# Order of two products, of a minimum and of two sums in the paired projections of a hybrid GLA and convolution block

## The chip, the cores and the metric

The kernel runs on one core of one Trainium2 chip. The metric is the device time of one execution in microseconds (us). The version before takes 891.07 us as the median of three runs (890.15 to 894.06).

## The reference

One layer on x of 1024 tokens by 1024 features: RMSNorm, one input projection, a gated linear attention group (4 heads, both directions) and a short convolution group side by side, one output projection, a residual and a last RMSNorm. Cut to what matters here:

```python
h = rmsnorm(x, norm_g)
q, k, v, z_a, lr_f, lr_b, b_gate, c_gate, h_c, z_c = split(h @ w_in)
g_f = log_sigmoid(lr_f @ w_gk_f + b_gk_f) / 16      # log decays; g_b alike
b = cumsum(g, within chunks of 64)                  # inside the attention
u = c_gate * h_c
conv = conv_w[0] * up[:, :-2] + conv_w[1] * up[:, 1:-1] + conv_w[2] * up[:, 2:] + conv_b
y_c = b_gate * conv * silu(z_c)
```

## The kernel before, in words

All matmuls work on float32 that is split in two parts: `split` (L153, L154) makes the high part as a cast on ScalarE (`a_hi`) and the low part as a subtraction on GpSimd (`a_lo`), and each product takes three matmuls (high by high, low by high, high by low). `part` allots the two tiles and calls `split`.

The projections go by **pairs**: `pair` takes two blocks of 128 columns of `w_in` (`raw0`, `raw1`, each 1024 x 128, loaded by `weights` at L82 from SP's queue into a pool of four buffers named `raw`) and makes both results (128 x 1024 each, in two halves of 512 tokens) by a scheme of seven products instead of eight: sums of quarters of the weights (`comb`, L422, on VectorE), their splits (`os1` to `os4`, `o11`), seven products with quarters and sums of the tokens' matrix (`b00`, `b10`, `b11`, `t1` to `t4`), and additions of the results (`plus`, L445, on VectorE from PSUM, and L458). Each finished half is handed to `take(e, half, ap)`. The products use three PSUM banks in turn, `pa`, `pb` and `pc`.

Two pairs make a **quad**: `second` first computes a smaller scheme of the same kind for both (L519 to L556) on half banks `bx`, `by`, `bz`, `bw`. In it the bank `by` is written by a first product, added to `p1` (L542) and then written again by a second product; `bx` is copied at L540 and then gets its second product. L526 to L530 are the sums of the weights that it needs, from the first raw blocks of both pairs.

After some stages for the attention's values (up to about 115 us) eight conv quads run, j from 0 to 7, and then four quads for q, k and z (up to about 600 us); attention and output projection follow. In conv quad j, pair a gives C and hc: `conv_u`'s `take` multiplies them on GpSimd to u (L625) as soon as both have the same half. Pair b gives z and B: at its first result both halves of the convolution are made (L633 on ScalarE, L634 and L635 on VectorE); z's halves go through a tanh (L647, ScalarE) and L648, L649 (VectorE), B's through a product on GpSimd (L651); the finished half is stored (L654).

At the end of conv quad j, `gates` makes the log decays of one head and direction: two small matmuls (L591) into a bank `out`, from there |x| (L592, ScalarE) and min(x, 0) (L593, VectorE), then Exp (L594). `summed` loads another activation table and takes Ln (L601), and puts five steps into the list `beside`: a subtraction (L611) and a scan (L605 or L607) for each half, and the store to `b_dram` (L613). `step`, called after each `plus` of pair a of the next quad, takes one step from the list and places it behind that addition.

The order of the instructions on each engine is not the order of the text: a scheduler sets it from the priorities and dependencies, and `tc.issue_after(x)` tells it to place what follows behind x. L396 is the matmul of `product`.

Of the kernel before, what the change touches and what calls it, by code (L numbers as in the profile page):

```python
# [2 lines left out]

# [11 lines left out]
ALU = mybir.AluOpType  # L15
# [3 lines left out]
P = 128  # L19
# [18 lines left out]
def tile_hybrid_gla_shortconv(ctx, tc, x, norm_g, w_in, w_gk_f, b_gk_f, w_gk_b, b_gk_b,  # L38
                              gla_norm_g, conv_w, conv_b, w_out, final_g, out):
    nc = tc.nc  # L40
    V, A, G, T = nc.vector, nc.scalar, nc.gpsimd, nc.tensor
# [18 lines left out]
    b_dram = [[dram.tile([P, S], F32, name=f"b_dram{h}{d}") for d in range(2)] for h in range(NH)]  # L60
# [146 lines left out]
    def part(src, e_lo=G, late=False):  # L207
        pool, name, bufs = (resp, "w", 2) if late else (ws, "a", 6)
        hi, lo = (pool.tile([P, 4, P], F32R, name=f"{name}_{i}", bufs=bufs) for i in ("hi", "lo"))
        hi, lo = (a[:, 0:src.shape[1]] for a in (hi, lo))  # L210
        split(hi, lo, src, A, e_lo)
        return hi, lo
# [20 lines left out]
    with tc.manual_schedule():  # L233
# [24 lines left out]
        for t in range(NT):  # L258
            ps = bank()[:, 0:DV]
# [13 lines left out]
            if t == 1:  # L273
                a00, a01 = (load_a(2, i) for i in range(2))
            if t in (5, 6):
                w_next.append(split_v(v_raw1[t - 5]))
            if t == 6:
                a10, a11 = (load_a(3, i) for i in range(2))
# [107 lines left out]
    def tmp():  # L386
        return wk.tile([P, 512], F32, name="tmp", bufs=9)
# [17 lines left out]
    def load(col):  # L405
        return weights(w_in[:, :, col:col + P])


    beside = []
# [4 lines left out]
            with tc.issue_after(behind.ins):  # L414
                beside.pop(0)()

    def pair(raw0, raw1, take, c2=None, mid=None, step=lambda behind: None):

        a00, a01, a10, a11 = raw0[:, 0:4], raw0[:, 4:8], raw1[:, 0:4], raw1[:, 4:8]

        def comb(f, x0, x1, op):
            V.tensor_tensor(f, x0, x1, op)  # L422
            return f

        def t4_():
            return tmp().rearrange("p (c e) -> p c e", e=P)

        o00 = part(a00)
        if c2 is None:
            o01 = part(a01)  # L430
        s1 = comb(s_tile(), a10, a11, ALU.add)
        s2 = comb(s_tile(), s1, a00, ALU.subtract)
        os2 = part(s2)
        os3 = part(comb(t4_(), a00, a10, ALU.subtract))
        os1 = part(s1)
        o11 = part(a11)
        os4 = part(comb(t4_(), a01, s2, ALU.subtract))

        def whole_product(a, b_):
            ps = bank6()  # L440
            product(ps, a, b_, True, True)
            return ps

        def plus(f, ps, x):
            step(V.tensor_tensor(f, ps, x, ALU.add))  # L445
            return f

        pa = whole_product(o00, b00)
        p1 = tmp()
        A.copy(p1, pa)  # L450
        if mid is not None:
            mid()
        if c2 is None:
            product(pa, o01, b10, False, True)
            c2 = tmp()
            A.copy(c2, pa)
        else:
            V.tensor_tensor(c2, pa, c2, ALU.add)  # L458
        take(0, 0, c2)
        plus(p1, whole_product(os2, t2), p1)  # L460
        w = plus(tmp(), whole_product(os3, t3), p1)
        p5 = whole_product(os1, t1)
        take(1, 1, plus(tmp(), p5, w))
        plus(p1, p5, p1)
        take(1, 0, plus(w, whole_product(o11, t4), w))
        take(0, 1, plus(p1, whole_product(os4, b11), p1))

    def value_pair(h0, h1, o00, o01, os2, a00, a01, a10, a11, s2, beside):

# [49 lines left out]
    def second(x, y, h):  # L519

        b00, t1, t2, t3, b10, b11, t4 = h
        a00, a01, a10, a11 = x[:, 0:2], x[:, 2:4], y[:, 0:2], y[:, 2:4]
        f, g = s_tile(), s_tile()
        s2, s1, s3, s4 = f[:, 0:2], f[:, 2:4], g[:, 0:2], g[:, 2:4]
        o0 = part(x)
        V.tensor_tensor(s1, a10, a11, ALU.add)  # L526
        V.tensor_tensor(s2, s1, a00, ALU.subtract)
        o1 = part(f)
        V.tensor_tensor(s3, a00, a10, ALU.subtract)
        V.tensor_tensor(s4, a01, s2, ALU.subtract)  # L530
        o2 = part(g)
        o3 = part(a11)
        first_, last_ = (lambda o: tuple(a[:, 0:2] for a in o)), (lambda o: tuple(a[:, 2:4] for a in o))
        r = [wk.tile([P, 512], F32, name="r2", bufs=2) for _ in range(2)]
        lo, hi = slice(0, 256), slice(256, 512)
        w = tmp()
        p1, u = w[:, lo], w[:, hi]
        bx, by, bz, bw = (bank6()[:, lo] for _ in range(4))
        product(bx, first_(o0), b00, True, True)
        A.copy(p1, bx)  # L540
        product(by, first_(o1), t2, True, True)
        V.tensor_tensor(p1, by, p1, ALU.add)  # L542
        product(bz, first_(o2), t3, True, True)
        V.tensor_tensor(u, bz, p1, ALU.add)
        product(bw, last_(o1), t1, True, True)
        V.tensor_tensor(r[1][:, hi], bw, u, ALU.add)
        product(bx, last_(o0), b10, False, True)
        A.copy(r[0][:, lo], bx)
        product(by, o3, t4, True, True)
        V.tensor_tensor(r[1][:, lo], by, u, ALU.add)  # L550

        def finish():
            product(bw, last_(o2), b11, False, True)
            V.tensor_tensor(r[0][:, hi], bw, p1, ALU.add)

        return *r, finish  # L556

    def quad(cols_a, take_a, cols_b, take_b):
        xa, xb = load(cols_a[0]), load(cols_b[0])
        ra, rb, finish = second(xa[:, 4:8], xb[:, 4:8], h2)  # L560
        pair(xa, load(cols_a[1]), take_a, ra, finish, step)
        pair(xb, load(cols_b[1]), take_b, rb)

    def to_dram(dsts):
# [17 lines left out]
    def gates(h, d):  # L582

        bias = bgk[:, d, h:h + 1]
        dr = slice(d * 64, d * 64 + 64)
        b, m = u_tile()[:, 0:S], u_tile()[:, 0:S]
        for half in range(2):
            sl = slice(half * 512, half * 512 + 512)
            ps = bank()
            for i, w in enumerate((gk_hi, gk_lo)):  # L590
                T.matmul(ps, w[dr, h * DK:(h + 1) * DK], lr[half][dr], start=i == 0, stop=i == 1)  # L591
            A.activation(b[:, sl], ps, AF.Abs, bias=bias)  # L592
            V.tensor_scalar(m[:, sl], ps, bias, 0.0, ALU.add, ALU.min)  # L593
        return b, m, A.activation(b, b, AF.Exp, scale=-1.0)  # L594

    def summed(h, d, b, m, exp):

        with tc.issue_after(exp.ins):  # L600
            A.activation(b, b, AF.Ln, bias=1.0)  # L601

        def scan(b_, m_):
            if d == 0:
                V.tensor_tensor_scan(b_, smask, m_, 0.0, ALU.mult, ALU.add)  # L605
            else:
                V.tensor_tensor_scan(b_[:, ::-1], smask, m_[:, ::-1], 0.0, ALU.mult, ALU.add)  # L607

        for half in range(2):
            b_, m_ = (a[:, half * 512:half * 512 + 512] for a in (b, m))  # L610
            beside.append(lambda b_=b_, m_=m_: V.tensor_tensor(m_, m_, b_, ALU.subtract))  # L611
            beside.append(lambda b_=b_, m_=m_: scan(b_, m_))
        beside.append(lambda: nc.sync.dma_start(b_dram[h][d], b))  # L613

    def conv_u(j):
        u = u_tile()
# [451 lines left out]
```

## Time and profile before

| | us |
|---|---|
| median of three runs | 891.07 (890.15 to 894.06) |
| the profiled execution | 889.61 |
| its span | 887.9 |
| TensorE (PE) busy | 860.0 (97%) |
| VectorE (DVE) busy | 704.4 (79%) |
| GpSimd (POOL) busy | 421.6 (47%) |
| ScalarE (ACT) busy | 393.7 (44%) |

The span is what the profiler recorded of the profiled execution; the 1.7 us around it belong to the same execution's time. Busy shares are averages over the whole span, which has stages of different kinds; what holds in a stage is read from windows and timelines of that stage. An idle time in square brackets behind a row tells how long the engine had been idle and what released it. The granted clock of TensorE was 0.995 of full speed over the execution.

### The profile page before, as it was taken

How to read it: one execution, taken by the hardware profiler on the slowest of the kernel's cores; microseconds unless marked ns; L12 is line 12 of the kernel's file. 1: busy time of each engine (PE TensorE's matmuls, PEld its weight loads, DVE VectorE, ACT ScalarE, POOL GpSimd, SP SyncE). 2: the span in 40 equal slices, each digit the busy share in tenths (PEclk: the TensorE clock that was granted, in tenths of full speed). 3: DMA queues.
4: the chain of work that ended last, by engine and by line, in shares of the span. 5: the costliest groups of instructions: out<-in, count | busy, mean ns of one | idle time of the engine just before them, and what ended most of it. 6: DMA issues, size and time to landing. Idle time of an engine off the chain costs nothing.

```text
span 887.9 us, 12975 instructions
## 1 busy us (share of the span) xinstructions
PE 860.0 (97%) x4452; PEld 722.8 (81%) x4452; DVE 704.4 (79%) x1301; ACT 393.7 (44%) x823; POOL 421.6 (47%) x374
## 2 busy tenths in 40 slices
PE   7999989999999999999999999999999999999996
PEld 6999978887787878788878888887878787888885
DVE  5889968788888798888887566667799989975754
ACT  4634323454636263444544233433455446542453
POOL 3423657586767675766766554520112222222231
PEclk9999999999999999999999999999999999999998
DMA  8511331223132322222244433469665434410122
GB/s 301 115 54 49 96 120 48 82 62 118 49 95 72 96 66 77 72 72 72 72 132 129 131 96 105 135 210 392 226 205 190 131 113 135 131 37 24 42 78 95
DMA packets 102164, 100.35 MB, mean 113 GB/s; under 512 B 10705, under 2 KB 82385, under 8 KB 101586
## 3 DMA queue, kind: packets, MB, share of 16 engines
q1 hardware_dynamic: 102098, 99.53, 35.4%
q8 instruction: 35, 0.57, 0.3%
q14 instruction: 31, 0.25, 0.1%
HBM read 71.20 MB, written 28.31 MB: 112 GB/s over the span
## 4 chain that ended last, share of the span: by engine, by line
PE 76%; DVE 17%; issue 3%; DMA 2%; ACT 1%; SPq 0%; POOLq 0%; POOL 0%; DVEq 0%; ACTq 0%
PE out L734 16%; PE pa L396 16%; PE pb L396 15%; PE pc L396 15%; PE po L891 4%; PE out L223 3%; PE pu L936 2%; DVE tmp L445 1%; DVE tmp L649 1%; DVE s L422 1%; DVE tmp L320 1%; DMA b<-b_dram 1%; PE out L291 1%; DMA xt<-in_x 1%; PE pk L928 1%
## 5 line engine op out<-in xcount | busy, mean ns | idle before, releaser
L154 POOL TENSOR_TENSOR a_lo<-s,a_hi 128x512 fp32r<-128x512 f32 x74 | 116.2, 1575 | 54.8 <-ACT a_hi L153 54.5
L154 POOL TENSOR_TENSOR a_lo<-raw,a_hi 128x512 fp32r<-128x512 f32 x84 | 111.0, 1325 | 22.1 <-ACT a_hi L153 18.4
L154 POOL TENSOR_TENSOR a_lo<-tmp,a_hi 128x512 fp32r<-128x512 f32 x48 | 70.3, 1464 | 103.9 <-ACT a_hi L153 84.6
L148 POOL TENSOR_TENSOR rs<-rs,mhalf 128x1 f32<-128x1 f32 x48 | 28.7, 598 | 143.1 <-DVE rs L147 135.7
L734 PE MATMUL out<-a_hi,y_hi 128*128 128x512 f32 x192 | 88.7, 462 | 0.5 <-ACT y_hi L153 0.5
L153 ACT CAST a_hi<-raw 128x512 fp32r<-128x512 f32 x108 | 63.8, 596 | 56.4 <-PE pc L396 15.1
L153 ACT CAST a_hi<-tmp 128x512 fp32r<-128x512 f32 x48 | 29.8, 620 | 120.2 <-DVE tmp L422 98.9
L734 PE MATMUL out<-a_hi,y_lo 128*128 128x512 f32 x192 | 77.0, 401 | 0.0
L734 PE MATMUL out<-a_lo,y_hi 128*128 128x512 f32 x192 | 76.8, 400 | 0.0
L846 POOL TENSOR_TENSOR kt<-kt,k 128x256 f32<-128x256 f32 x32 | 26.3, 822 | 95.5 <-ACT kt L843 72.2
L153 ACT CAST a_hi<-s 128x512 fp32r<-128x512 f32 x74 | 45.0, 617 | 50.7 <-PE pa L396 17.5
L396 PE MATMUL pb<-h_hi,a_hi 128*128 128x512 f32 (+1 forms) x128 | 48.3, 377 | 4.8 <-DVE tmp L542 4.2
L396 PE MATMUL pc<-h_hi,a_hi 128*128 128x512 f32 (+1 forms) x128 | 47.6, 372 | 2.9 <-DVE tmp L542 2.6
L396 PE MATMUL pa<-h_hi,a_hi 128*128 128x512 f32 (+1 forms) x128 | 47.6, 372 | 2.8 <-DVE tmp L542 2.8
L396 PE MATMUL pb<-h_lo,a_hi 128*128 128x512 f32 (+1 forms) x128 | 47.1, 368 | 0.0
L396 PE MATMUL pb<-h_hi,a_lo 128*128 128x512 f32 (+1 forms) x128 | 47.0, 367 | 0.0
L396 PE MATMUL pa<-h_lo,a_hi 128*128 128x512 f32 (+1 forms) x128 | 46.6, 364 | 0.0
L396 PE MATMUL pc<-h_lo,a_hi 128*128 128x512 f32 (+1 forms) x128 | 46.6, 364 | 0.0
L396 PE MATMUL pc<-h_hi,a_lo 128*128 128x512 f32 (+1 forms) x128 | 46.5, 363 | 0.0
L396 PE MATMUL pa<-h_hi,a_lo 128*128 128x512 f32 (+1 forms) x128 | 46.5, 363 | 0.0
L736 DVE TENSOR_TENSOR res<-out,res 128x512 f32<-128x512 f32 x48 | 32.9, 686 | 12.4 <-PE out L734 12.4
L734 PEld LDWEIGHTS out<-a_hi,y_lo 128*128 128x128 f32 x192 | 36.3, 189 | 7.8
(341 smaller groups left out, 2696.6 us busy)
## 6 DMA issues: line engine op xcount, KB each, us to landing
raw<-in_w_in SPq DMA_DIRECT2D x56, 512.0 KB, 3.9
raw<-in_w_out SPq DMA_DIRECT2D x16, 512.0 KB, 3.8
xt<-in_x SPq DMA_DIRECT2D x8, 512.0 KB, 8.2
yc_dram<-tmp SPq DMA_DIRECT2D x16, 256.0 KB, 2.0
b_dram<-u SPq DMA_DIRECT2D x8, 512.0 KB, 2.6
z_dram<-tmp SPq DMA_DIRECT2D x16, 256.0 KB, 2.6
s<-yc_dram SPq DMA_DIRECT2D x16, 256.0 KB, 3.9
raw<-in_x SPq DMA_DIRECT2D x8, 512.0 KB, 6.3
```

The costliest lines, as they stand in the source:

```text
L148: G.tensor_tensor(rs, rs, mhalf, ALU.pow)
L153: (e_hi.copy if e_hi is A else e_hi.tensor_copy)(hi, src)
L154: e_lo.tensor_tensor(lo, src, hi.bitcast(F32), ALU.subtract)
L223: last_mm[0] = T.matmul(ps, h_tile(a, c, t), wv[c // 4][w_][:, c % 4, :], start=part == 0 and c == 0, stop=part == 2 and c == ND - 1)
L291: T.matmul(lps, lrw[:, c, :], hb[c // 4][half][j][:, c % 4, :], start=c == 0 and j == 0, stop=c == ND - 1 and j == 1)
L320: V.tensor_tensor(f, blk[0].bitcast(F32)[:, c], blk[1].bitcast(F32)[:, c], ALU.add)
L396: T.matmul(ps, a[x0][:, k], b_[x1][:, k], start=start and k == 0 and j == 0, stop=stop and k == n - 1 and j == 2, skip_group_check=not start)
L734: T.matmul(ps, a[:, j, :], w, start=j == 0 and i == 0, stop=j == 3 and i == 2)
L736: V.tensor_tensor(res[t][:, cs], ps, (xr if row0 == NT else res[t])[:, cs], ALU.add)
L846: G.tensor_tensor(kk, kk, k4, ALU.mult)
L891: T.matmul(o, l, m, start=j == 0, stop=j == len(mm) - 1)
L936: T.matmul(pu[:, d], ks[:, d], r["v"][:, t], start=True, stop=True)
```

## The change

Three edits in the code of the pairs.

1. In `pair`, os4 is made ahead of o11, and its product with b11 ("p3", which gives `take(0, 1)`) ahead of o11's product with t4 ("p4", which gives `take(1, 0)`).
2. `second` returns the addition L542 as `added`; in pair a of each quad the sums for os3 and os4 are placed behind it with `tc.issue_after`.
3. In `gates` the two minima are no longer issued at once; each becomes a step of `beside`, ahead of the subtractions and scans. The store to `b_dram` joins the last scan's step, so that there are six steps for the six additions.

```diff
-    def pair(raw0, raw1, take, c2=None, mid=None, step=lambda behind: None):
+    def pair(raw0, raw1, take, c2=None, mid=None, step=lambda behind: None, behind=None):
...
-        def t4_():
-            return tmp().rearrange("p (c e) -> p c e", e=P)
+        def later(x0, x1):
+            with tc.issue_after(behind.ins) if behind is not None else nullcontext():
+                return comb(tmp().rearrange("p (c e) -> p c e", e=P), x0, x1, ALU.subtract)
...
-        os3 = part(comb(t4_(), a00, a10, ALU.subtract))
+        os3 = part(later(a00, a10))
         os1 = part(s1)
+        os4 = part(later(a01, s2))
         o11 = part(a11)
-        os4 = part(comb(t4_(), a01, s2, ALU.subtract))
...
         plus(p1, p5, p1)
+        take(0, 1, plus(p1, whole_product(os4, b11), p1))
         take(1, 0, plus(w, whole_product(o11, t4), w))
-        take(0, 1, plus(p1, whole_product(os4, b11), p1))
...
-        V.tensor_tensor(p1, by, p1, ALU.add)
+        added = V.tensor_tensor(p1, by, p1, ALU.add)
...
-        return *r, finish
+        return *r, finish, added
...
-        ra, rb, finish = second(xa[:, 4:8], xb[:, 4:8], h2)
-        pair(xa, load(cols_a[1]), take_a, ra, finish, step)
+        ra, rb, finish, added = second(xa[:, 4:8], xb[:, 4:8], h2)
+        pair(xa, load(cols_a[1]), take_a, ra, finish, step, added)
...
-            V.tensor_scalar(m[:, sl], ps, bias, 0.0, ALU.add, ALU.min)
+            beside.append(lambda m_=m[:, sl], ps=ps: V.tensor_scalar(m_, ps, bias, 0.0, ALU.add, ALU.min))
...
-        beside.append(lambda: nc.sync.dma_start(b_dram[h][d], b))
+        last = beside.pop()
+        beside.append(lambda: (last(), nc.sync.dma_start(b_dram[h][d], b)))
```

Lines move by 1 to 3: L422 becomes L423, L445 L447, L526 L528, L540 L542, L542 L544, L592 L594, L593 L595, L611 L613, L625 L628, L633 L636, L634 L637, L647 L650, L648 L651, L649 L652, L651 L654.

What the change moves on VectorE at the end of a conv quad (`th` is z's tanh, `pa` to `pc` are banks, L542 is the addition that PE waits for). Before:

```order
L422 TENSOR_TENSOR s<-raw 128x512
L445 TENSOR_TENSOR tmp<-pa,tmp 128x512 x2
L445 TENSOR_TENSOR tmp<-pb,tmp 128x512
L445 TENSOR_TENSOR tmp<-pc,tmp 128x512
L593 TENSOR_SCALAR u<-out,bgk 128x512
L648 SCALAR_TENSOR_TENSOR th<-th,tmp 128x512
L593 TENSOR_SCALAR u<-out,bgk 128x512
L649 SCALAR_TENSOR_TENSOR tmp<-th,tmp 128x512
L542 TENSOR_TENSOR tmp<-pb,tmp 128x256
```

The same place after:

```order
L423 TENSOR_TENSOR s<-raw 128x512
L447 TENSOR_TENSOR tmp<-pa,tmp 128x512 x2
L447 TENSOR_TENSOR tmp<-pb,tmp 128x512
L651 SCALAR_TENSOR_TENSOR th<-th,tmp 128x512
L652 SCALAR_TENSOR_TENSOR tmp<-th,tmp 128x512
L447 TENSOR_TENSOR tmp<-pc,tmp 128x512
L544 TENSOR_TENSOR tmp<-pb,tmp 128x256
```

The two minima have left, and the last addition of the pair has moved behind the two instructions on the tanh.

On ScalarE at the same place (L153 is the cast of a split, L592 the Abs of the gates, L647 the tanh). Before:

```order
L153 CAST a_hi<-raw 128x512
L153 CAST a_hi<-s 128x512
L592 ACTIVATE u<-out,bgk 128x512
L647 ACTIVATE th<-tmp 128x512
L592 ACTIVATE u<-out,bgk 128x512
L540 COPY tmp<-pb 128x256
L594 ACTIVATE u<-u 128x1024
```

After:

```order
L153 CAST a_hi<-raw 128x512
L650 ACTIVATE th<-tmp 128x512
L153 CAST a_hi<-s 128x512
L594 ACTIVATE u<-out,bgk 128x512 x2
L542 COPY tmp<-pb 128x256
L596 ACTIVATE u<-u 128x1024
```

The tanh now stands ahead of one cast and of both Abs.

On GpSimd in pair a of a conv quad (L154 is the low part of a split; `tmp` there is os3 or os4, `s` os1, `raw` o11 or a first block; L625 makes u, from `r` for the first half of the tokens). Before:

```order
L154 TENSOR_TENSOR a_lo<-tmp,a_hi 128x512
L154 TENSOR_TENSOR a_lo<-s,a_hi 128x512
L154 TENSOR_TENSOR a_lo<-raw,a_hi 128x512
L154 TENSOR_TENSOR a_lo<-tmp,a_hi 128x512
L154 TENSOR_TENSOR a_lo<-raw,a_hi 128x512
L154 TENSOR_TENSOR a_lo<-s,a_hi 128x512
L154 TENSOR_TENSOR a_lo<-tmp,a_hi 128x512
L625 TENSOR_TENSOR u<-r_2980,tmp 128x512
L154 TENSOR_TENSOR a_lo<-s,a_hi 128x512
L154 TENSOR_TENSOR a_lo<-raw,a_hi 128x512
L154 TENSOR_TENSOR a_lo<-tmp,a_hi 128x512
L625 TENSOR_TENSOR u<-tmp 128x512
```

After:

```order
L154 TENSOR_TENSOR a_lo<-tmp,a_hi 128x512
L154 TENSOR_TENSOR a_lo<-s,a_hi 128x512
L154 TENSOR_TENSOR a_lo<-tmp,a_hi 128x512
L154 TENSOR_TENSOR a_lo<-raw,a_hi 128x512 x2
L154 TENSOR_TENSOR a_lo<-s,a_hi 128x512
L154 TENSOR_TENSOR a_lo<-tmp,a_hi 128x512
L628 TENSOR_TENSOR u<-tmp 128x512
L154 TENSOR_TENSOR a_lo<-s,a_hi 128x512
L154 TENSOR_TENSOR a_lo<-tmp,a_hi 128x512
L154 TENSOR_TENSOR a_lo<-raw,a_hi 128x512
L628 TENSOR_TENSOR u<-r_2978,tmp 128x512
```

os4's low part stands ahead of o11's in both pairs, and the half of u that comes from `r` is now the last.

## Rows read from the trace of the kernel before

**Rows 1.** The page, busy us of each engine (share of the span) and its instructions.

```profile
PE 860.0 (97%) x4452; PEld 722.8 (81%) x4452; DVE 704.4 (79%) x1301; ACT 393.7 (44%) x823; POOL 421.6 (47%) x374
```

**Rows 2.** Seven conv quads by window: its length, busy us of each engine, PEclk, DMA.

```profile
154.82:195.05 40.23, 39.52 (x191) 32.67 (x190) 32.72 (x44) 18.77 (x31) 27.98 (x22) 1.00 0.27 79
195.05:235.49 40.44, 39.52 (x192) 32.70 (x191) 34.69 (x45) 18.84 (x31) 29.21 (x22) 1.00 0.27 79
...
sum 284.97, PE 277.94 PEld 229.10 DVE 240.91 ACT 131.83 POOL 203.09; mean PE 39.70 PEld 32.73 DVE 34.42 ACT 18.83 POOL 29.01
```

**Rows 3.** What PE waits for from 154 to 460 us: total, times, longest.

```profile
PE pa L396 <- DVE tmp L542: 2.8, 3, 1.0
PE pc L396 <- DVE tmp L542: 2.6, 3, 1.0
PE pb L396 <- DVE tmp L542: 1.9, 2, 1.0
```

**Rows 4.** Timeline of ACT in one conv quad: start us, us, instruction, idle before.

```profile
197.45 0.63 ACT L647 ACTIVATE th<-tmp 128x512 f32<-128x512 f32 x1 [0.95 <-DVE tmp L445]
...
202.41 0.62 ACT L153 CAST a_hi<-tmp 128x512 fp32r<-128x512 f32 x1
202.93 0.62 ACT L153 CAST a_hi<-s 128x512 fp32r<-128x512 f32 x1
...
238.20 0.63 ACT L647 ACTIVATE th<-tmp 128x512 f32<-128x512 f32 x1 [1.27 <-DVE tmp L445]
...
238.74 0.67 ACT L592 ACTIVATE u<-out,bgk 128x512 f32<-128x512 f32 x1
```

**Rows 5.** Timeline of POOL in the same quad.

```profile
203.11 1.31 POOL L154 TENSOR_TENSOR a_lo<-tmp,a_hi 128x512 fp32r<-128x512 f32 x1 [1.37 <-ACT a_hi L153]
...
206.08 1.29 POOL L154 TENSOR_TENSOR a_lo<-raw,a_hi 128x512 fp32r<-128x512 f32 x1
...
218.37 1.55 POOL L154 TENSOR_TENSOR a_lo<-tmp,a_hi 128x512 fp32r<-128x512 f32 x1 [6.77 <-ACT a_hi L153]
...
225.74 1.74 POOL L625 TENSOR_TENSOR u<-tmp 128x512 f32<-128x512 f32 x1
```

**Rows 6.** Timeline of SP's queue, 207 to 208 us.

```profile
207.40 0.38 SPq L82 DMA_DIRECT2D raw<-in_w_in  x1
```

**Rows 7.** Timeline of DVE in the same quad.

```profile
208.74 1.71 DVE L611 TENSOR_TENSOR u<-u 128x512 f32<-128x512 f32 x1
...
211.34 0.54 DVE L526 TENSOR_TENSOR s<-raw 128x256 f32<-128x256 f32 x1 [0.90 <-DMA raw<-in_w_in]
...
212.86 1.21 DVE L607 TENSOR_TENSOR_SCAN u<-smask,u 128x512 f32<-128x512 f32 x1
...
214.57 0.68 DVE L611 TENSOR_TENSOR u<-u 128x512 f32<-128x512 f32 x1
...
216.90 0.67 DVE L422 TENSOR_TENSOR tmp<-raw 128x512 f32<-128x512 f32 x1
...
228.36 0.93 DVE L634 SCALAR_TENSOR_TENSOR tmp<-u,cw,tmp 128x512 f32<-128x512 f32 x1 [2.04 <-ACT tmp L633]
...
237.49 0.68 DVE L445 TENSOR_TENSOR tmp<-pc,tmp 128x512 f32<-128x512 f32 x1
...
241.19 0.41 DVE L542 TENSOR_TENSOR tmp<-pb,tmp 128x256 f32<-128x256 f32 x1
```

**Rows 8.** Groups of DVE by line, 154.82 to 439.79 us: busy, mean ns, idle.

```profile
L593 DVE TENSOR_SCALAR u<-out,bgk 128x512 f32<-128x512 f32 x14 | 10.3, 739 | 0.6 <-ACT u L592 0.6
...
L526 DVE TENSOR_TENSOR s<-raw 128x256 f32<-128x256 f32 x7 | 3.5, 505 | 7.2 <-DMA raw<-in_w_in 6.0 <-POOL a_lo L154 1.2
```

**Rows 9.** What PE waits for from 100 to 154 us.

```profile
PE pb L396 <- DVE tmp L542: 2.3, 1, 2.3
```

**Rows 10.** Timeline of DVE at the first conv quad.

```profile
117.23 0.68 DVE L422 TENSOR_TENSOR tmp<-raw 128x512 f32<-128x512 f32 x1
...
118.43 0.41 DVE L542 TENSOR_TENSOR tmp<-pb,tmp 128x256 f32<-128x256 f32 x1
```

More of the change, by code (lines that the diff above doesn't have):

```diff
@@ L1 @@
-from contextlib import ExitStack
+from contextlib import ExitStack, nullcontext
 from itertools import chain
```

## The prediction

> **What bounds the kernel now.** I read the busy times first, then the conv quads by windows, then what TensorE (PE) waits for in them, then the timelines of the other engines. PE is busy for 97% of the span [rows 1], and the seven windows of a conv quad each show the same: they sum to 284.97 us, of which PE works 277.94, so 39.70 us of work stand in a period of 40.7 us [rows 2]. One microsecond of every quad is idle, and nearly all of it has one releaser: PE waits for L542, the addition that frees `by` for its second product. From 154 to 460 us these waits take 2.8 + 2.6 + 1.9 = 7.3 us in eight waits of at most 1.0 us each [rows 3]. That is what the page offers at first sight: remove 1.0 us ahead of L542 and PE would run through.
>
> The timelines say that it is not a mere queue. Follow one tanh (L647, of pair b, at 197.45) to the next one (238.20) [rows 4]. ScalarE (ACT) works on through the second Abs, L540, Exp, the table load, Ln and L548 and reaches the cast of pair a's os3 at 202.41: 4.96 us. GpSimd (POOL) makes its low part from 203.11 [rows 5], 0.70 later, then without a pause those of os1 and o11, and the one of o11 ends at 206.08 + 1.29 = 207.37: 4.26. With that the buffer of a raw block is free, and SP issues the load of the next one at 207.40 [rows 6]: 0.03. VectorE (DVE) has to wait for that load in L526, which starts at 211.34 after 0.90 idle [rows 7]: 3.94. Behind L526 the queue runs full to the sum for pair b's os3 at 216.90: 5.56. POOL, idle for 6.77 before, starts on its low part at 218.37: 1.47; four items later, at 225.74, the second half of u (L625) begins: 7.37. ACT's L633 and then DVE's second L634 wait for it; that starts at 228.36 after 2.04 idle: 2.62. From there DVE has no pause up to the next tanh at 238.20: 9.84. The sum is 40.75 us, and that is the period of rows 2. So the conv quads are bounded by **a ring through ACT, POOL, a load and DVE**, 1.05 us longer than PE's work; PE's wait for L542 is only where the ring's lateness shows. L526 waits for its load in the other quads too: 6.0 us of DMA waits in seven [rows 8].
>
> **The change, term by term.** Each is costed on that ring, once per conv quad.
>
> - *(a) ACT.* In the order of before only one Abs and L540 stood between the tanh and Exp. Now the tanh comes one product earlier in ACT's order, and the cast of an s and both Abs stand behind it. The cast takes a step of 0.52 (202.41 to 202.93), one more Abs at most its 0.67 [rows 4]: +1.1. Lower end +0.5, if the Abs would have found ACT idle; upper +1.2.
> - *(b) The load.* The part of os4 now goes ahead of the part of o11, on ACT and on POOL; o11's low part is what frees the raw buffer. POOL runs without a pause there, so the load is issued later by one low part, 1.31 in the row of 203.11 [rows 5]: +1.3. L526 already waits for that load, so nothing covers it; both ends are 1.3.
> - *(c) DVE between L526 and the sum for os3.* Before, two scans and one subtraction lay there; with six steps instead of five, and the first one a minimum, it is a minimum, a subtraction and one scan. A scan of 1.21 [rows 7] goes, a minimum of 0.739 [rows 8] comes: -0.5. The other minimum takes the place of the subtraction ahead of L526, where DVE waits anyway. The upper end is +0.5: the subtraction takes 1.71 at 208.74 and 0.68 at 214.57 [rows 7], and it could be the long one.
> - *(d) u.* p3 ahead of p4 turns round the halves: the second half of u comes first, and the first half last. L633 and L634 of the first half stand first in their queues, so both halves now wait for the last L625, where one L634 was done before it. One more L634 behind it: +0.9 (0.93 at 228.36) [rows 7]; lower end 0, if other work of DVE fills the wait.
> - *(e) The tanh* is released by the last L445 but one instead of the last (0.68 at 237.49) [rows 7]: -0.6; upper end 0.
>
> The minimum's removal from the end of the quad (two of 0.739, so 1.48 less ahead of L542) is real, but it is not on the ring: both stand behind the L445 that releases the tanh. L542 starts 2.99 us after the tanh (238.20, 241.19) [rows 4, 7]; now the tanh itself, L648, L649 and the last L445 lie between the two, about as much, so L542 moves with the ring. Where the minima are done now is counted in (c). The later place of the two sums for os3 and os4 changes only the first quad and those of q and k, since a conv quad had L542 ahead of them already; in the first quad PE waits 2.3 us for L542 [rows 9], which stands behind two sums from 117.23 to 118.43 [rows 10], and of that wait 1.2 go. The swap of the two products alone costs PE nothing: they have the same number of matmuls.
>
> Sum per quad: 1.1 + 1.3 - 0.5 + 0.9 - 0.6 = **+2.2 us**, so a period of about 43. Seven periods give 15.4; the last tanh's delay goes into the first q and k quad with (a) alone, +1.1; the first quad gives back 1.2. Together +15.3. The profiled run took 889.61 us, which becomes 904.9; the median of the three runs lies 1.46 above the profiled run, so I say **906 us**. By the ends, the lowest sum is 0.5 + 1.3 - 0.5 + 0 - 0.6 = 0.7 a quad, some +5 in all (896), the highest 1.2 + 1.3 + 0.5 + 0.9 - 0 = 3.9, some +27 (918).
>
> A rule bears on (c). The subtraction took 1.71 us while POOL was at work and 0.68 while POOL stood idle [rows 5, 7]. The Trainium skill, "SBUF — State Buffer", section "Who interferes with whom", says that a DVE instruction with two SBUF inputs contends with a GpSimd instruction that reads SBUF, because both use one read interface; the trace agrees in these two rows. By it the price of (c) depends on whether the delayed POOL chain still runs when the subtraction comes: -0.5 if not, +0.5 if so.
>
> **The rivals.**
>
> *Rival A, faster.* PE's 1.0 us is just a queue: DVE issues two minima of 0.739 between the last L445 and L542, 1.48 in all, more than the stall. Without them all waits on L542 close, 7.3 us, and 1.2 of the first quad: 889.61 - 8.5 = 881.1, on the median 882.6. It decides if the ring has over 2.2 us of slack somewhere, so that ACT, POOL and the load can come later unnoticed. For it: DVE is without a pause ahead of L542, and the minima stand there. Against it: the links sum to the period with each start given by the one before, and L526 and L634 stand waiting [rows 7]. The Trainium skill, "Perfetto Trace Analysis", section "Optimization Strategy", tells to look for the gaps of the engine that one optimizes, find what blocks it there and make that start sooner; followed on PE alone that is this rival. Chance 0.10.
>
> *Rival B, no change.* The gain ahead of L542 and the new delays cancel: only (c), (d), (e), the earlier L542 (-1.48) and the later Abs (two steps of 0.67 on ACT) meet, -0.5 + 0.9 - 0.6 - 1.48 + 1.34, which is about 0 (-0.3); the load's delay (b) would have to hide. About 890. Against it: L526's wait of 0.90 shows the load as last. Chance 0.07.
>
> *Rival C, slower still.* The same ring, with the subtraction contended, as in the 1.71 row: 3.2 a quad, 22.4 in seven, +22.3 in all, 912 on the profiled run and 913.4 on the median. For it: two more items of POOL's lie where DVE adds in SBUF. Chance 0.19.
>
> That the change doesn't do what it says I exclude: the new order of each engine shows all three moves.
>
> **How the numbers follow.** The forecast has 0.64. About 0.5% (4.5 us) can be told from no change here. Slower by more: forecast and rival C, 0.83; the same: rival B, 0.07; faster: rival A, 0.10. The range reaches from 895 (lower ends) to 917 (rival C and most of the upper ends); with A and B outside it leaves out about 2 in 10.
>
> **What would show it.** In the profile after: the period of a conv quad at 43 instead of 40.7, with PE's work of 39.7 unchanged; 3 to 4 us of PE's idle time in each, with new waits for L540's copy (now L542) because the Abs stand ahead of it, of some 2 us, and with waits for the addition (now L544) still there; DVE still waiting for a load at L526 (now L528); both L633 behind the last product of u; a wait of 1.1 on the addition in the first quad, where 2.3 was. The step on the ring is wrong if the period falls to 39.7 and DVE's wait at the load vanishes; (b) is wrong if the load is issued as early after the cast of os3 as now (5 us); (d) if the first L634 still goes out before the last L625.

## The result, and the profile after

The changed kernel takes 914.22 us (median of four runs, 913.37 to 916.62), the kernel before 892.57 us beside it: a ratio of 1.0241, 95% interval 1.021 to 1.0272, so 21.65 us slower. The forecast was 906 us with a range of 895 to 917.

The profiled execution took 914.49 us (span 912.8) against 889.61 us. Page, part 1 of the changed kernel:

```profile
PE 870.1 (95%) x4452; PEld 729.4 (80%) x4452; DVE 710.2 (78%) x1301; ACT 390.2 (43%) x823; POOL 421.8 (46%) x374
```

TensorE (PE) is busy for a smaller share than in [rows 1], and VectorE's (DVE) share falls too: every engine waits more. Windows of the changed kernel from one z tanh to the next (length, busy us of each engine, PEclk, DMA share, GB/s):

```profile
153.61:197.35 43.74, 43.00 (x216) 35.64 (x214) 36.38 (x45) 18.52 (x30) 29.11 (x23) 1.00 0.25 72
197.35:242.51 45.16, 42.11 (x188) 34.43 (x188) 36.49 (x45) 18.62 (x31) 29.07 (x23) 0.92 0.25 71
242.51:286.27 43.76, 40.52 (x196) 33.23 (x194) 36.35 (x45) 18.52 (x31) 29.09 (x23) 1.00 0.26 73
286.27:330.02 43.75, 40.84 (x190) 33.64 (x189) 36.40 (x45) 18.61 (x30) 28.99 (x23) 0.96 0.26 73
330.02:375.63 45.61, 42.63 (x192) 34.95 (x192) 35.28 (x45) 18.62 (x30) 29.24 (x23) 0.93 0.25 70
375.63:420.39 44.76, 42.45 (x190) 34.87 (x189) 36.37 (x45) 18.61 (x30) 29.06 (x23) 0.92 0.25 71
420.39:464.33 43.94, 40.52 (x196) 33.24 (x194) 36.32 (x45) 18.53 (x30) 29.10 (x23) 1.00 0.24 73
```

Where PE's clock is granted in full, a conv quad takes 43.76 us (242.51 to 286.27), where the ring of the prediction came to 40.75. In four of the seven the granted clock is under 1.00, and three of these are longer by 1.0 to 1.9 us. What PE waits for from 154 to 480 us in the changed kernel:

```profile
PE pc L396 <- ACT tmp L542: 7.0, 3, 2.4
PE pb L396 <- ACT tmp L542: 4.4, 2, 2.4
PE pa L396 <- ACT tmp L542: 4.1, 2, 2.2
PE pc L396 <- DVE tmp L544: 1.6, 3, 0.8
```

The waits for the addition [rows 3] have shrunk to 0.8 us each, and the larger part now names the copy (L540, now L542): ScalarE (ACT) does both Abs ahead of it. The addition itself starts 3.94 us behind the tanh in the quad from 242.51 (2.99 before); the prediction put it at "about as much".

**The whole account** comes from the start times of the addition (L542, now L544), which DVE does once per quad. The first addition of a conv quad is 0.66 us earlier than before (117.77 for 118.43), the second 1.75 more; the seven periods from the second to the ninth take 310.66 us (157.58 to 468.24) for 285.69 (159.99 to 445.68), +24.97; the three quads of q, k and z up to the twelfth take +1.72 (115.87 for 114.15). The sum is +24.28 of the 24.9 us that the span is longer; the rest comes later.

**The ring after**, in the quad from 242.51 to 286.27, to be held against [rows 4 to 7]. ACT (start us, us, instruction):

```profile
242.51 0.63 ACT L650 ACTIVATE th<-tmp 128x512 f32<-128x512 f32 x1 [5.62 <-DVE tmp L447]
243.04 0.60 ACT L153 CAST a_hi<-s 128x512 fp32r<-128x512 f32 x1
243.55 1.26 ACT L594 ACTIVATE u<-out,bgk 128x512 f32<-128x512 f32 x2
...
248.56 0.62 ACT L153 CAST a_hi<-tmp 128x512 fp32r<-128x512 f32 x1
...
286.27 0.63 ACT L650 ACTIVATE th<-tmp 128x512 f32<-128x512 f32 x1 [5.62 <-DVE tmp L447]
```

GpSimd (POOL); the row of 253.49 is two low parts of o11 and of the next block, so o11's ends at about 254.8; SP issues the load at 254.82:

```profile
249.26 1.31 POOL L154 TENSOR_TENSOR a_lo<-tmp,a_hi 128x512 fp32r<-128x512 f32 x1 [1.30 <-ACT a_hi L153]
...
253.49 2.55 POOL L154 TENSOR_TENSOR a_lo<-raw,a_hi 128x512 fp32r<-128x512 f32 x2
...
265.23 1.55 POOL L154 TENSOR_TENSOR a_lo<-tmp,a_hi 128x512 fp32r<-128x512 f32 x1 [7.94 <-ACT a_hi L153]
...
271.35 2.21 POOL L154 TENSOR_TENSOR a_lo<-raw,a_hi 128x512 fp32r<-128x512 f32 x1
273.53 1.75 POOL L628 TENSOR_TENSOR u<-r,tmp 128x512 f32<-128x512 f32 x1
```

DVE:

```profile
254.15 0.69 DVE L447 TENSOR_TENSOR tmp<-pc,tmp 128x512 f32<-128x512 f32 x1 [1.54 <-PE pc L396]
...
258.77 0.43 DVE L528 TENSOR_TENSOR s<-raw 128x256 f32<-128x256 f32 x1 [3.27 <-DMA raw<-in_w_in]
...
263.76 0.67 DVE L423 TENSOR_TENSOR tmp<-raw 128x512 f32<-128x512 f32 x1
...
270.75 1.72 DVE L607 TENSOR_TENSOR_SCAN u<-smask,u 128x512 f32<-128x512 f32 x1
...
276.17 0.93 DVE L637 SCALAR_TENSOR_TENSOR tmp<-u,cw,tmp 128x512 f32<-128x512 f32 x1 [1.45 <-ACT tmp L636]
```

Link by link, in us:

| link | before | after | difference | forecast |
|---|---|---|---|---|
| tanh to the cast of pair a's os3 (ACT) | 4.96 | 6.05 | +1.09 | (a) +1.1 |
| cast to its low part (POOL) | 0.70 | 0.70 | 0 | 0 |
| low part to the first sum of `second`, through the load | 8.23 | 9.51 | +1.28 | (b) +1.3 |
| that sum to the sum for pair b's os3 (DVE) | 5.56 | 4.99 | -0.57 | (c) -0.5 |
| sum to its low part | 1.47 | 1.47 | 0 | 0 |
| low part to the last product of u (POOL) | 7.37 | 8.30 | **+0.93** | 0 |
| u to the step of the convolution that waits for it (DVE) | 2.62 | 2.64 | +0.02 | 0 |
| from there to the tanh | 9.84 | 10.10 | +0.26 | (d) and (e) together: +0.3 |
| sum | 40.75 | 43.76 | +3.01 | +2.2 |

The five terms came as forecast; the sixth link was forecast at nothing. There POOL does the same six items as before, in another order, but its low part of a raw block takes 2.21 us at 271.35, while DVE's scan (270.75) takes 1.72. In the kernel before that low part took 1.29, and the last scan lay ahead of POOL's whole chain, which began at 218.37 [rows 5]. Timelines of POOL, then of DVE, before:

```profile
222.76 1.29 POOL L154 TENSOR_TENSOR a_lo<-raw,a_hi 128x512 fp32r<-128x512 f32 x1
```

```profile
215.77 1.21 DVE L607 TENSOR_TENSOR_SCAN u<-smask,u 128x512 f32<-128x512 f32 x1
```

**The clock.** PE in the quad from 197.35, windows of 2 us:

```profile
198.00:200.00 2.00, 0.03 (x1) 0.03 (x1) 1.88 (x2) 2.00 (x5) 1.90 (x2) 1.00 0.00 0
...
202.00:204.00 2.00, 2.00 (x8) 1.84 (x9) 2.00 (x3) 1.99 (x5) 0.77 (x3) 0.50 0.37 144
...
208.00:210.00 2.00, 2.00 (x13) 1.75 (x12) 1.07 (x2) 1.55 (x3) 1.72 (x3) 1.00 0.00 0
```

PE stands still from 197.6 to 199.97, a wait of 2.41 us for the copy, and the granted clock falls from 1.00 (2.4 GHz) to 0.50 (1.2 GHz); it is back at 208. In the next quad the same wait is 1.96 us, and the clock stays at 1.00. The length of the longest wait alone does not tell such quads apart: in e5 below no wait is over 2.0 us, and six of the seven windows are granted 0.92 to 0.96. Timeline of PE in both quads:

```profile
199.97 0.38 PE L396 MATMUL pc<-h_hi,a_hi 128*128 128x256 f32 x1 [2.41 <-ACT tmp L542]
```

```profile
245.12 0.38 PE L396 MATMUL pa<-h_hi,a_hi 128*128 128x256 f32 x1 [1.96 <-ACT tmp L542]
```

In the quad from 197.35, DVE then waits for PE between the load and the sum for os3, and that link takes 6.04 us instead of 4.99. Timeline of DVE there:

```profile
217.07 0.69 DVE L447 TENSOR_TENSOR tmp<-pa,tmp 128x512 f32<-128x512 f32 x1 [0.96 <-PE pa L396]
```

Seven full-clock periods of 43.76 would be 306.32 us; the seven additions' periods took 310.66, so some 4.3 us lie beyond them, most in the three long quads at a lower clock. No run changes the clock alone, so this is read from the rows and not tested by itself.

### The profile page after: what moved, and what is told of

Same layout as the page of the kernel before. It is cut to its first block, busy times and chain, and to the rows that moved or that the text cites. A ratio compares the mean times of both kernels' runs of the same rounds, so it can differ in the third digit from the quotient of the medians.

```text
span 912.8 us, 12978 instructions
## 1 busy us (share of the span) xinstructions
PE 870.1 (95%) x4452; PEld 729.4 (80%) x4452; DVE 710.2 (78%) x1301; ACT 390.2 (43%) x823; POOL 421.8 (46%) x374
## 4 chain that ended last, share of the span: by engine, by line
PE 66%; DVE 20%; DMA 5%; issue 4%; ACT 2%; POOL 1%; SPq 1%; DVEq 0%; POOLq 0%; ACTq 0%
PE out L737 15%; PE pa L396 14%; PE pb L396 13%; PE pc L396 13%; PE po L894 3%; DVE tmp L447 3%; PE pu L939 2%; DVE s L423 1%; DVE th L651 1%; DMA lr_w<-in_w_in 1%; DMA raw<-in_w_in 1%; PE out L223 1%; DVE tmp L320 1%; DMA k<-k_dram 1%; DVE tmp L637 1%
## 5 line engine op out<-in xcount | busy, mean ns | idle before, releaser
L154 POOL TENSOR_TENSOR a_lo<-s,a_hi 128x512 fp32r<-128x512 f32 x74 | 111.1, 1508 | 64.2 <-ACT a_hi L153 63.4
L154 POOL TENSOR_TENSOR a_lo<-raw,a_hi 128x512 fp32r<-128x512 f32 x84 | 117.4, 1409 | 21.2 <-ACT a_hi L153 17.5
L154 POOL TENSOR_TENSOR a_lo<-tmp,a_hi 128x512 fp32r<-128x512 f32 x48 | 68.4, 1424 | 113.9 <-ACT a_hi L153 109.4
L153 ACT CAST a_hi<-raw 128x512 fp32r<-128x512 f32 x108 | 62.8, 595 | 53.6 <-issue 18.7
L153 ACT CAST a_hi<-tmp 128x512 fp32r<-128x512 f32 x48 | 29.8, 620 | 118.2 <-DVE tmp L423 112.8
L153 ACT CAST a_hi<-s 128x512 fp32r<-128x512 f32 x74 | 44.7, 615 | 32.1 <-PE pa L396 10.5
L396 PE MATMUL pa<-h_hi,a_hi 128*128 128x512 f32 (+1 forms) x128 | 50.7, 396 | 7.2 <-ACT tmp L542 5.6
L396 PE MATMUL pa<-h_lo,a_hi 128*128 128x512 f32 (+1 forms) x128 | 49.2, 384 | 0.0
L396 PE MATMUL pa<-h_hi,a_lo 128*128 128x512 f32 (+1 forms) x128 | 49.2, 384 | 0.0
```

The source lines that it names most:

```text
L153: (e_hi.copy if e_hi is A else e_hi.tensor_copy)(hi, src)
L154: e_lo.tensor_tensor(lo, src, hi.bitcast(F32), ALU.subtract)
L396: T.matmul(ps, a[x0][:, k], b_[x1][:, k], start=start and k == 0 and j == 0, stop=stop and k == n - 1 and j == 2, skip_group_check=not start)
```

## The experiments

Theories to tell apart: the ring of the prediction, with its terms; the naive reading, by which PE's waits (for the addition, the minima ahead of it, or the copy) are themselves the cost; and what came up on the way. All ratios are to the kernel before, run on the same chip.

**e1 to e4: the edits undone or alone.** The diffs of e1 to e3 are against the change. e1:

```diff
-        os4 = part(later(a01, s2))
         o11 = part(a11)
+        os4 = part(later(a01, s2))
...
-        take(0, 1, plus(p1, whole_product(os4, b11), p1))
         take(1, 0, plus(w, whole_product(o11, t4), w))
+        take(0, 1, plus(p1, whole_product(os4, b11), p1))
```

> The change with its first edit undone (os4 behind o11 and p4 ahead of p3 again; minima as steps and the sums behind the addition kept). Ring theory: terms (a), (b), (d), (e) go, (c) stays, so the ring is 40.75 - 0.5 = 40.2 us; seven quads give -3.8, the first quad's earlier addition -1.2, the addition one minimum earlier after the tanh -0.6: about 887 us on a before of 892.6, ratio 0.993 to 0.996. Rival (the minima among the steps, or the two sums behind the addition, cost the time): the ratio stays over 1.01. Rival A of the prediction (PE's wait is a mere queue behind the minima): all waits on the addition go, 884 or less.

Measured: 905.64 us (900.58 to 911.33), ratio 1.0138 (1.0084 to 1.0193). About 887 was expected, so this is a miss by some 18 us: the minima among the steps (with the two sums) cost 1.4% by themselves, where the whole change costs 2.4%. The full-clock quad from 244.57 to 286.74 takes 42.17 us. Timelines of POOL, then of DVE, in it:

```profile
265.38 2.15 POOL L154 TENSOR_TENSOR a_lo<-tmp,a_hi 128x512 fp32r<-128x512 f32 x1 [7.08 <-ACT a_hi L153]
...
270.38 2.21 POOL L154 TENSOR_TENSOR a_lo<-raw,a_hi 128x512 fp32r<-128x512 f32 x1
...
274.27 1.74 POOL L628 TENSOR_TENSOR u<-tmp 128x512 f32<-128x512 f32 x1
```

```profile
265.09 0.68 DVE L613 TENSOR_TENSOR u<-u 128x512 f32<-128x512 f32 x1
...
269.78 1.72 DVE L607 TENSOR_TENSOR_SCAN u<-smask,u 128x512 f32<-128x512 f32 x1
```

Term (c) is there (4.99 to 5.12 us for 5.56 in the full-clock quads but the first), but the way from os3's low part to the last u is 8.89 us (8.28 to 8.89 in the seven quads), for 7.37 before. The minima take the first two steps, so each subtraction and scan comes two additions later than before. Before, all four stood ahead of the sum at 216.90 (the last of them at 215.77, shown above), and POOL, idle until then, began its chain at 218.37 [rows 5, 7]. Now the second subtraction (265.09) and the second scan (269.78) lie beside that chain; the scan is 1.72 us long where it took 1.21 [rows 7], and POOL's low parts next to the two take 2.15 and 2.21.

e2 and e3 each undo one half of edit one: e2 only the order of the parts, e3 only that of the products, as in the diff above.

> The change with only the order of the parts undone (o11's part ahead of os4's again; product p3 ahead of p4 kept). Ring theory: (b) goes, 1.25 us a quad, so a ring of 43.76 - 1.25 = 42.5 and, with shorter idle times of PE, no stretch at the lower clock (4 us of the change's time): 900 to 906 us. If the load is not on the ring: unchanged at 914.

Measured: 916.58 us, ratio 1.025 (1.0208 to 1.0293), the same as the change. Term (b) does go from its link, but nothing comes of it: in the quad from 153.62 the first sum of `second` starts 15.03 us behind the tanh instead of 16.26, and the sum for os3 21.15 us behind it instead of 21.25. Timelines of PE, then of DVE, in that quad of e2:

```profile
164.87 0.39 PE L396 MATMUL pa<-t_hi,a_lo 128*128 128x512 f32 x1
```

```profile
168.65 0.43 DVE L528 TENSOR_TENSOR s<-raw 128x256 f32<-128x256 f32 x1 [4.89 <-DMA raw<-in_w_in]
168.99 0.68 DVE L447 TENSOR_TENSOR tmp<-pa,tmp 128x512 f32<-128x512 f32 x1
...
174.77 0.67 DVE L423 TENSOR_TENSOR tmp<-raw 128x512 f32<-128x512 f32 x1
```

What the earlier load gave, **DVE's own queue** took back. PE's product in `pa` ends at 165.26, but its addition (168.99) stands behind the sum that waits for the load, and so does a minimum; in the change both were done during that wait (254.15). From the load to the sum for os3 DVE now works 6.12 us without a pause, where it was 4.99.

There is also **a second way** from the tanh to that sum: the addition L544 is queued behind the two instructions on the tanh, PE's products wait for it (and for the copy behind the Abs), and the additions of their results stand ahead of the sum on DVE. It is nearly as long as the way through the load. In the kernel before, DVE takes up such a result 0.41 us after PE's product has ended (213.19 + 0.39, then 213.99), and in this quad of e2 1.1 us after it, so in neither does it hold the sum. Timelines of PE, then of DVE, before:

```profile
213.19 0.39 PE L396 MATMUL pa<-t_hi,a_lo 128*128 128x512 f32 x1
```

```profile
213.99 0.67 DVE L445 TENSOR_TENSOR tmp<-pa,tmp 128x512 f32<-128x512 f32 x1
```

> The change with only the order of the products undone (p4 ahead of p3 again; os4's part ahead of o11's kept). Ring theory: (a), (d), (e) go, (b) and (c) stay: ring 40.75 + 1.25 - 0.5 = 41.5, up to 42.4 if GpSimd's contended low part of 2.21 us ahead of u stays; 7 x 0.75 to 7 x 1.65, less 1.8: 896 to 903 us. If only the parts' order matters: 914; if only the products' order matters: 887.

Measured: 911.21 us, ratio 1.0206 (1.0158 to 1.0254), slower than the 896 to 903 that were expected. The quad from 330.44 to 373.35, at a clock of 1.00, takes 42.91: 4.96 to the cast as before, 9.54 through the load as in the change, 4.99 to the sum for os3, and again 8.27 on POOL from os3 to u. Quads at 0.92 to 0.96 take up to 44.8, and the first of the seven takes 44.28 at a clock of 1.00.

> The first edit alone on the kernel before (p3 ahead of p4 with os4's part ahead of o11's; minima at the end of the quad as before, sums not tied to the addition). Ring theory: (a) + (b) + (d) + (e) and the 0.93 us more on GpSimd ahead of u, without (c): ring 44.3; 892.6 + 7 x 3.5 + 1.1 = 918, and some 4 to 8 us of stretches at the lower clock: 918 to 926 us, slower than the whole change. If the minima among the steps cost time: faster than the whole change, under 912.

The diff of e4, against the kernel before, is the swap of e1 the other way round, in both places. Measured: 918.47 us, ratio 1.0275 (1.0239 to 1.0311), as expected: edit one alone is as slow as the whole. POOL's way from os3 to u is 7.36 to 7.38 us in all seven quads there, so the longer way belongs to the steps and not to edit one. The two parts do not add up: 2.75% here and 1.4% in e1 against 2.4% together. In e4, where the minima still stand ahead of the addition, it starts 5.2 to 5.3 us behind the tanh, in the change 3.9 to 4.0; that this is why the change costs less than the sum is not tested.

**e5: the copy ahead of the Abs.** Against the change, the Abs of the gates wait in ACT's queue for the copy of the next quad (the rest keeps its order on every engine but for two memsets):

```diff
-        A.copy(p1, bx)
+        copied = A.copy(p1, bx)
+        if hook:
+            hook.pop()(copied)
...
+                with tc.issue_after(copied.ins):
+                    A.activation(b[:, sl], ps, AF.Abs, bias=bias)
```

> The change with the copy L540 (L542 after) placed ahead of both Abs on ScalarE, all else in the same order. Naive reading of PE's waits (18.3 us... of the change's waits name this copy; it comes 1.15 us earlier in eight quads): about 9 us faster, 905. Ring theory: Exp, the table and Ln stand behind the Abs as before, so the ring is still 43.76 us; PE's idle time moves from the copy to the addition; the period at the full clock stays within 0.2 of 43.76, and at most the stretches at the lower clock (4 us) go, if the longest idle time falls under 2.4 us: 909 to 915.

Measured: 914.86 us, ratio 1.0243 (1.021 to 1.0276), the same as the change. PE's waits in e5, 154 to 480 us (the addition is L550 here, the copy L546):

```profile
PE pa L396 <- DVE tmp L550: 5.2, 3, 2.0
PE pc L396 <- DVE tmp L550: 4.2, 3, 2.0
PE pb L396 <- DVE tmp L550: 4.0, 2, 2.0
PE pc L396 <- ACT tmp L546: 3.3, 3, 1.3
```

The waits for the copy have changed their name to waits for the addition. The periods (43.99 to 44.93) are not shorter; my figure of 43.76 within 0.2 was a little low, and the stretches at the lower clock did not go, although no wait is over 2.0 us. Window of e5, one quad:

```profile
287.38:331.37 43.99, 40.75 (x188) 33.48 (x187) 36.49 (x45) 18.73 (x30) 29.06 (x23) 0.96 0.26 72
```

**e6 to e8: o11's part first.** In each, `o11 = part(a11)` moves ahead of os3's line: e6 in the change, e7 in the kernel before, e8 in e1.

```diff
+        o11 = part(a11)
         os3 = part(comb(t4_(), a00, a10, ALU.subtract))
         os1 = part(s1)
-        o11 = part(a11)
```

> The change with the part of o11 made first, ahead of os3, os1 and os4 (so that the raw buffer is free earlier), nothing else. Ring theory: three low parts (1.31 + 1.76 + 1.30 = 4.3 us) leave the way to the load, the ring falls to some 39.5 and PE's own 39.7 bound the quad: 914 - 7 x 4.06 - 4 = 882, at worst 890 if another ring of 40.5 stands behind it. If the load is not on the ring: 914.

Measured: 901.29 us, ratio 1.0102 (1.0069 to 1.0135). 13 us faster than the change, so the load is on the ring; but 882 to 890 was expected, and the period is 42.0: in the quad from 196.62 the first sum of `second` starts 13.2 us behind the tanh instead of 16.26, but the sum for os3 20.6 instead of 21.25. Again DVE works without a pause between the two, 7.4 us for the 4.99 of the change: one more addition and one more minimum stand behind the load, and its second sum takes 1.40 us where it took 0.42. PE's products were ready 0.66 us or more before their additions, so the second way does not hold the sum here.

> The kernel before with the part of o11 made first, ahead of os3 and os1. Ring theory: 3.0 us leave the way to the load, so the ring no longer binds and the period falls from 40.75 to PE's 39.7: -7 us, 883 to 886, and VectorE no longer waits for the raw load at the first sum of second. If PE's wait was a queue behind the minima (rival A): no change.

Measured: 889.73 us, ratio 0.9963 (0.9939 to 0.9987). The period falls to 40.54, not to 39.7. VectorE did not stop waiting for its load: it is idle for 2.9 us up to 211.63 in the quad from 199.64. The load is 1.9 us earlier behind the tanh (11.99 for 13.89), but from there DVE works 8.45 us without a pause to the sum for os3, where it was 5.56: an addition whose product had ended at 210.26 and a subtraction stand behind the load now. The sum comes 1.0 us later (20.43 behind the tanh for 19.45), and the way from it to the next tanh is 1.2 shorter, since POOL has only 5.66 us from os3's low part to u. All products were ready 1.4 us or more before their additions. So the 40.54 is the way through the load with a longer queue behind it, and no measure of the second way; the expectations of e10 to e12 take it for one.

> Edits two and three (minima as steps, sums behind the addition), the first undone, and the part of o11 made first. Ring theory: PE bounds the quads at 39.7 and the first quad's wait is 1.2 shorter: 881 to 885, at least as fast as the kernel before with o11 first.

Measured: 891.71 us, ratio 0.9979 (0.9954 to 1.0004), period 41.16. Expected were 881 to 885, a miss: the steps beside POOL's chain make it 7.18 us long for e7's 5.66 here too, and the period is 0.6 longer than e7's.

**e9: the steps put back.** Against e1, both minima go into the first step, so that the subtractions and scans keep their old places:

```diff
-            beside.append(lambda m_=m[:, sl], ps=ps: V.tensor_scalar(m_, ps, bias, 0.0, ALU.add, ALU.min))
+            mins.append(lambda m_=m[:, sl], ps=ps: V.tensor_scalar(m_, ps, bias, 0.0, ALU.add, ALU.min))
...
-        last = beside.pop()
-        beside.append(lambda: (last(), nc.sync.dma_start(b_dram[h][d], b)))
+        beside.append(lambda: nc.sync.dma_start(b_dram[h][d], b))
+        ms, f = mins[:], beside[0]
+        mins.clear()
+        beside[0] = lambda: (ms[0](), ms[1](), f())
```

> As e1 (edits two and three, the first undone), but both minima go into the first step together with the first subtraction, so that the subtractions and scans keep the places they had before. Theory of the contended steps: with six steps the last subtraction and scan lie beside GpSimd's chain from pair b's os3 to u and lengthen it from 7.4 to 8.3 to 8.9 us in e1 and in the change; here it is 7.4 again, the period 40.7, and the time 0.996 to 1.001 of the kernel before (890). If the minima themselves, or the two sums behind the addition, cost the time: the chain may be 7.4, but the time stays near e1's 905.

Measured: 889.13 us, ratio 0.9968 (0.9951 to 0.9984), 1.7% or about 15 us under e1 by the two ratios. Timeline of POOL in its quad from 196.02, the rows that answer to those of e1:

```profile
216.97 1.56 POOL L154 TENSOR_TENSOR a_lo<-tmp,a_hi 128x512 fp32r<-128x512 f32 x1 [7.26 <-ACT a_hi L153]
...
221.38 1.30 POOL L154 TENSOR_TENSOR a_lo<-raw,a_hi 128x512 fp32r<-128x512 f32 x1
...
224.35 1.74 POOL L630 TENSOR_TENSOR u<-tmp 128x512 f32<-128x512 f32 x1
```

The way is 7.38 us again, the low part of the raw block 1.30, the period 40.80. The work is the same as in e1; only the steps have other places (each subtraction and scan two additions earlier). That shows that their place beside POOL's chain, and not the minima or the sums behind the addition, is what edits two and three cost.

Here the second way does bind: in this quad DVE comes to the load's sum (L528) without idle time, and the wait that is left is for PE. Timeline of DVE:

```profile
206.68 0.69 DVE L447 TENSOR_TENSOR tmp<-pb,tmp 128x512 f32<-128x512 f32 x1 [1.52 <-PE pb L396]
...
210.19 0.41 DVE L528 TENSOR_TENSOR s<-raw 128x256 f32<-128x256 f32 x1
```

**e10 to e12: both ways cut.** e10, against the kernel before, keeps the last half's instructions on the tanh back until the next quad's addition (`late` is a list; `rest` holds L648, L649 and the store):

```diff
+            if (e, half) == (0, 1):
+                late.append(rest)
+            else:
+                rest()
...
+        added = V.tensor_tensor(p1, by, p1, ALU.add)
+        if late:
+            with tc.issue_after(added.ins):
+                late.pop()()
```

> The kernel before with the two instructions on the last tanh (L648, L649 and the store behind them) placed behind the addition L542 that PE waits for. If PE's wait were the bound (naive): the addition comes 1.4 us earlier, more than the wait of 1.0, and the time falls by 7 to 8 us, 885. Two-way theory (a way through ScalarE, GpSimd and the load, 40.75, and one through the addition and PE, 40.5, as e7 shows): only the second is cut, the period stays at 40.5 to 40.75, and the time within 2 us of the kernel before.

Measured: 893.23 us, ratio 1.0016 (0.9997 to 1.0036): no change. PE hardly waits for the addition in the conv quads any more, and yet the quads take 40.97. PE's waits in e10, 154 to 480 us:

```profile
PE pc L396 <- ACT tmp L540: 4.4, 3, 1.7
PE pa L396 <- ACT tmp L540: 2.7, 2, 1.3
PE pb L396 <- ACT tmp L540: 2.6, 2, 1.3
```

The wait that the page offers first is gone and the time is not: DVE waits 2.1 to 2.2 us for the load in six of the seven quads, up from 0.9 in [rows 7].

> e10 and e7 together: the two instructions on the tanh behind the addition, and o11's part first. Two-way theory: both ways are now under PE's own 39.7 us, so the period falls to 39.7 to 39.9 and the time by 6 to 8 us, 885 (0.992), though e7 alone gave 0.5 a quad at most; more than the sum of e7 and e10 where e10 gives nothing. If a third way stands at 40.5: no better than e7 (889).

Measured: 885.16 us, ratio 0.9926 (0.9903 to 0.995); the period is 40.03. e7 alone gave 0.4% and e10 nothing; together they give 0.7%. With the addition earlier, the first of PE's products for pair a ends 9.6 us behind the tanh (238.34) where it took 10.6 in e7, its addition and a subtraction stand ahead of the load again, and the sum for os3 comes 19.9 us behind the tanh where it was 20.4. The period stays 0.3 over PE's own work.

> e9 with o11's part first and the two instructions on the tanh behind the addition (edits two and three in their place, edit one undone). Two-way theory: period 39.7 as in e11, and the first quad's wait 1.2 us shorter: 883 to 885. If the contended chain returns: 8.3 us from pair b's os3 to u, period over 40.

Measured: 881.05 us (880.34 to 882.17), ratio 0.9877 (0.9853 to 0.9902): faster than both kernels, and 2 us under what was expected, though the period is 40.1 as in the window below and not 39.7. The 4 us that it gains on e11 lie outside the seven quads: its first tanh here stands at 154.57, that of e11 at 157.76. Window of e12, one quad:

```profile
235.40:275.50 40.10, 39.46 (x192) 32.63 (x191) 36.57 (x45) 18.94 (x30) 30.03 (x23) 1.00 0.28 79
```

## Why the prediction was right, and where it was not

- **The bound.** Right: the quads are bounded by a ring, not by PE's queue. e5 and e10 remove the wait that PE names and change nothing; e6 and e7 shorten the load's way and gain. That the ring is one way was too simple: from the tanh to the sum for pair b's os3 a second way runs through the addition and PE, by the rows only 0.4 us shorter in the kernel before, and it binds in e9. Nor is a link's gain kept: what DVE did while it waited for the load comes behind the load when that is earlier (e2, e6, e7).
- **Terms (a), (b), (d) and (e).** Each link moved as forecast (+1.09, +1.28, and +0.26 for the two last). But a term undone alone can give nothing: e2 took (b) out, DVE's queue behind the load grew by 1.1 us, and the time stayed that of the change. (b) is a true length of its way and not a price that can be got back by itself.
- **Term (c)**, "a scan of 1.21 goes, a minimum of 0.739 comes: -0.5", is right for the link (-0.57) and wrong as the price of the steps. This is the term of the sum that was mis-sized: the steps that left this link turn up two additions later, one subtraction and one scan of them beside POOL's chain from os3 to u, and lengthen it by 0.93 (1.5 in some quads). With it edits two and three cost 1.4% by themselves (e1), against the small gain that the terms gave. Rival C had a contended subtraction as its mechanism and 913.4 us as its time, and came nearest, in part by luck: it put the price on DVE's subtraction, and the traces show it on POOL's low parts, and it had nothing for the clock.
- **The rule in (c).** The Trainium skill, "SBUF — State Buffer", section "Who interferes with whom", says that a DVE instruction with two SBUF inputs and a GpSimd instruction that reads SBUF hold each other off, and that the order of issue decides which one waits. The traces agree that the two slow each other: low part 2.21 us beside a scan of 1.72 in the changed kernel and e1, and 1.30 and 1.21 apart in e9. Which of them waits by the order of issue no run here tests. I had applied it to one instruction on DVE only, and only upwards to +0.5.
- **The clock** was not in the prediction at all: behind waits of PE of 2.2 to 2.4 us the granted clock was 0.50 for 3 to 7 us in four of the seven quads, and three of these took 1.0 to 1.9 us more, about 4.3 in all.
- **First quad and end.** The wait of 2.3 us in the first quad is 1.1, as forecast, and the second addition comes 1.75 earlier still, which I had not counted (the ring had not closed by then). The q, k and z quads took +1.72, where +1.1 was forecast.

The forecast of +2.2 a quad became +3.0 by the contended steps, and about 4.3 us came with the clock: 7 x 0.8 + 4.3 is 9.9, about the 9.6 by which the seven periods passed their forecast (24.97 for 15.4). The other differences nearly cancel: +0.5 in the first quad, -1.75 in the second, +0.6 in those of q, k and z, +0.6 after them. So the direction and five terms came by the mechanism; that 914.2 still lies under the upper end of 917 is partly luck, since that end was made up of other costs. Rival A (faster) and rival B fell: nothing on the ring had the slack that they needed.

## What to carry to other kernels

Where the waits of the busy engine all have the same length in every turn, follow one instruction through to its next turn and add up the links before costing an edit; an edit that removes the wait but no link gives nothing (e10), and one that brings a load forward can lose most of it again to the work that the waiting engine now does behind the load (e2, e7), while an earlier load and earlier results of PE together pay (e11, e12). Work moved "beside" something must be placed against the other engines' chains too: the same subtractions and scans, two additions later, cost about 15 us (e1 against e9).

## What the runs showed of the hardware

A scan on VectorE and a subtraction on GpSimd, both from SBUF, that overlapped took 1.72 and 2.21 us (changed kernel, e1) where they took 1.21 and 1.30 apart (e9). In the changed kernel TensorE, idle for 2.41 us, was granted 0.50 of its clock from about 201 to 207 us; after idle times of 1.96 and 0.81 us in the next quad it kept 1.00. In e5, with no idle time over 2.0 us, it was granted 0.92 to 0.96 in six of seven quads.
